# Sums of the modulation weights: three GpSimd instructions a tile, or two on VectorE

## The chip, the core and the metric

The kernel runs on one core of a Trainium2 chip. The metric is the device time of one execution in microseconds (us); smaller is better. A core has TensorE (PE, matrix products; PEld is its loading of weights), VectorE (DVE), ScalarE (ACT), GpSimd (POOL), and SyncE (SP), whose queue issues nearly all transfers here. Each engine takes its own instructions in order; engines wait for each other by semaphores.

## What is computed

A transformer of four layers (attention of three kinds, a memory attention, SwiGLU) runs over 256 positions, and behind it a second block of two layers. The second block scales, shifts and gates its layers by a modulation vector, which depends on a small input c alone:

```python
c_act = jax.nn.silu(c.astype(jnp.float32))          # 1 x 1024
def hybrid_layer(x, c_act, norm_g, w_ada, b_ada, w_in, w_out, pos):
    mod = c_act @ w_ada + b_ada                     # w_ada: 1024 x 3072, for each of two layers
    shift, scale, gate = jnp.split(mod, 3, axis=-1)
    h = rms_norm(x, norm_g) * (1.0 + scale[:, None, :]) + shift[:, None, :]
    ...
```

The change concerns the product c_act @ w_ada.

## The kernel before

All weights are fp32 and pass through the core once. `load_w` (L249) loads a tile of 128x1024 (512 KB) into a buffer `raw` (a pool of 5 buffers), splits it into a high part `wh` (ACT, L262) and a low part `wl` (DVE, L264), and PE multiplies with both (three products each). `wh` and `wl` have eight buffers each; a buffer is free when PE has used it.

A layer of the first block goes through projections and attention, the out projection with a layer norm (`add_norm`: L481 and L482 on DVE sum and take statistics, L455 and L448 give v, L450 on POOL takes its power -1/2, L462 and L463 on DVE apply it; PE then transposes the result in L368), gate and up in six groups (`units_T`, L436 to L438, eight weight tiles in each but the first; ACT applies silu in L1135, DVE multiplies with up in L1139, ACT and DVE split the product in L1142 and L1143), and down (L295 to L297). Down takes over accumulator banks, one of which is free only when L1139 has read it.

The modulation is computed on the side, during gate and up of the four layers. w_ada is loaded in 48 tiles `raw` of 256 rows by 512 columns (kq is the tile's number in a chunk of four, ch the chunk, of which there are six to each of two modulation layers). In the order of loads two such tiles follow each of the six gate and up groups. `load_ada` (L1205) issues the load on SP, and POOL multiplies both halves of the tile with silu(c), one value to each partition, and adds them to the chunk's sum `ada`:

```python
cb = self.cact[:, kq * 2:kq * 2 + 2].unsqueeze(2).to_broadcast([P, 2, 512])
nc.gpsimd.tensor_tensor(rv, rv, cb, op=ALU.mult)                     # L1216
if kq == 0:
    nc.gpsimd.tensor_tensor(acc, rv[:, 0, :], rv[:, 1, :], op=ALU.add)    # L1218
else:
    nc.gpsimd.tensor_tensor(acc, acc, rv[:, 0, :], op=ALU.add)       # L1220
    nc.gpsimd.tensor_tensor(acc, acc, rv[:, 1, :], op=ALU.add)       # L1221
```

After a chunk's fourth tile, DVE transposes and reduces the sum (L1227, L1228). The buffer `raw` is free for the next load when the last reader has ended; SP takes its loads in order, so one that waits for a buffer holds those behind it. A scheduler orders each engine's instructions by its own estimate when the program is built.

Of the kernel before, what the change touches and what calls it, by code (L numbers as in the profile page):

```python
# [15 lines left out]
ALU = mybir.AluOpType  # L16
AX = mybir.AxisListType

P = 128
# [101 lines left out]
class _Net:  # L121
# [1083 lines left out]
    def load_ada(self, l, ch, kq):  # L1205

        nc, I = self.nc, self.I
        c0 = ch * 512
        if kq == 0:
            self.ada_acc = self.s2([512], name="ada")  # L1210
        acc = self.ada_acc
        raw = self.rawp.tile([P, 1024], F32, name="raw", tag="t")
        rv = raw.rearrange("p (k n) -> p k n", n=512)
        nc.sync.dma_start(rv, I["w_ada_2"][l, kq * 256:kq * 256 + 256, c0:c0 + 512].rearrange("(k p) n -> p k n", p=P))
        cb = self.cact[:, kq * 2:kq * 2 + 2].unsqueeze(2).to_broadcast([P, 2, 512])
        nc.gpsimd.tensor_tensor(rv, rv, cb, op=ALU.mult)  # L1216
        if kq == 0:
            nc.gpsimd.tensor_tensor(acc, rv[:, 0, :], rv[:, 1, :], op=ALU.add)  # L1218
        else:
            nc.gpsimd.tensor_tensor(acc, acc, rv[:, 0, :], op=ALU.add)  # L1220
            nc.gpsimd.tensor_tensor(acc, acc, rv[:, 1, :], op=ALU.add)  # L1221
        if kq < 3:
            return

        def finish():
            t = self.s2([512], name="adaT")
            nc.vector.transpose(t, acc)  # L1227
            nc.vector.tensor_reduce(self.adared[l][:, ch * 16:ch * 16 + 16], t.rearrange("p (b i) -> p b i", i=32),  # L1228
                                    axis=AX.X, op=ALU.add)
            if ch < 5:  # L1230
                return
            ps = self.at_bank()
            nc.tensor.matmul(ps[0:32, 0:96], self.fold, self.adared[l], start=True, stop=True)
            col = self.adain[l]
            nc.vector.tensor_tensor(col, ps[0:32, 0:96], col, op=ALU.add)
            scale = col[:, 32:64]
            nc.vector.scalar_tensor_tensor(scale, scale, 1.0, self.adag[l], op0=ALU.add, op1=ALU.mult)
            nc.sync.dma_start(self.rows[l].rearrange("o (k p) -> p (o k)", p=32), col)

        self.put_off(12, finish)  # L1240
# [349 lines left out]
```

## Time and profile before

| | |
|---|---|
| runs | 1643.12 us median of 3 (1642.08 to 1646.56) |
| profiled execution | 1647.93 us, its span 1646.2 us |
| PE, matrix products | busy 1589.9 us, 97% of the span |
| DVE | 1119.7 us, 68% |
| ACT | 825.2 us, 50% |
| POOL | 390.6 us, 24% |
| granted clock of TensorE | 0.989 of 2.4 GHz over the span |
| transfers | 299.98 MB, 182 GB/s in the mean |

The profile comes from one execution. Times in it count from the start of the span. A wait is put down to the instruction that ended last before the waiting one could go on. A busy share is a mean over parts with different limits, so what counts for the time is which engine waits in which part, and for whom.

### The profile page before, as it was taken

The numbers are of one execution on the slowest core, as the hardware profiler recorded it, in microseconds if no ns is written. First come the engines' busy times: TensorE is split into PE (matmuls) and PEld (weight loads), VectorE is DVE, ScalarE is ACT, GpSimd is POOL, SyncE is SP. The second block draws the span as 40 slices with busy tenths as digits, with TensorE's granted clock in tenths as the row PEclk, the third lists the DMA queues.
The fourth block names the chain that finished last, engine by engine and source line by source line (L and its number), as shares of the span: only waits on it lengthen the run. The fifth ranks groups of instructions, "written<-read, shape, count | busy, mean of one in ns | idle before, by whom it ended". The sixth has DMA issues, their size and how long they took to land.

```text
span 1646.2 us, 27453 instructions
## 1 busy us (share of the span) xinstructions
PE 1589.9 (97%) x10840; PEld 1427.3 (87%) x10840; DVE 1119.7 (68%) x1496; ACT 825.2 (50%) x1281; POOL 390.6 (24%) x358
## 2 busy tenths in 40 slices
PE   8899999999999998999999999999999899999997
PEld 7788799978889998889799988887999778887976
DVE  7963777757567876575578847865788566486475
ACT  5575544444454443366444534655444345655572
POOL 2210343401122442022335500123254011001002
PEclk9999999999999999999999999999999999999999
DMA  8736477655456665663366666533676567344721
GB/s 288 213 110 198 147 251 240 216 182 170 126 166 192 229 224 194 179 191 124 123 220 212 240 211 216 150 103 122 219 239 233 146 202 268 102 154 145 226 78 39
DMA packets 200529, 299.98 MB, mean 182 GB/s; under 512 B 26576, under 2 KB 84304, under 8 KB 200400
## 3 DMA queue, kind: packets, MB, share of 16 engines
q1 hardware_dynamic: 200400, 298.23, 56.7%
q8 instruction: 85, 1.39, 0.3%
q14 instruction: 44, 0.36, 0.1%
HBM read 295.54 MB, written 2.65 MB: 181 GB/s over the span
## 4 chain that ended last, share of the span: by engine, by line
PE 44%; DVE 3%; DMA 2%; POOL 2%; ACT 2%; issue 1%; POOLq 0%; SPq 0%; ACTq 0%; DVEq 0%
PE mm L295 7%; PE mm L296 7%; PE mm L297 7%; PE mm L438 6%; PE mm L437 6%; PE mm L436 6%; PE at L368 2%; DVE wl L264 1%; DMA raw<-w_ada 1%; DMA raw<-w_down 1%; PE at L810 1%; ACT wh L262 1%; PE at L1388 1%; POOL raw L1216 0%; PE at L1401 0%
## 5 line engine op out<-in xcount | busy, mean ns | idle before, releaser
L264 DVE TENSOR_TENSOR wl<-raw,wh 128x1024 fp32r<-128x1024 f32 (+2 forms) x488 | 656.8, 1360 | 310.4 <-ACT wh L262 298.6
L262 ACT ACTIVATE wh<-raw 128x1024 fp32r<-128x1024 f32 (+2 forms) x488 | 509.5, 1048 | 528.1 <-DMA raw<-w_gate_up 201.9
L436 PE MATMUL mm<-xh,wh 128*128 128x256 f32 x1472 | 416.9, 283 | 0.0
L438 PE MATMUL mm<-xh,wl 128*128 128x256 f32 x1472 | 416.6, 283 | 0.0
L437 PE MATMUL mm<-xl,wh 128*128 128x256 f32 x1472 | 416.5, 283 | 0.0
L295 PE MATMUL mm<-wh,xh 128*128 128x256 f32 (+3 forms) x912 | 294.6, 324 | 1.7 <-ACT xh L408 1.7
L296 PE MATMUL mm<-wl,xh 128*128 128x256 f32 (+3 forms) x912 | 289.4, 318 | 2.3 <-DVE wl L264 2.3
L297 PE MATMUL mm<-wh,xl 128*128 128x256 f32 (+3 forms) x912 | 288.3, 317 | 0.0
L437 PEld LDWEIGHTS mm<-xl,wh 128*128 128x128 f32 x1472 | 282.6, 192 | 0.1
L436 PEld LDWEIGHTS mm<-xh,wh 128*128 128x128 f32 x1472 | 282.6, 192 | 0.1
L438 PEld LDWEIGHTS mm<-xh,wl 128*128 128x128 f32 x1472 | 282.6, 192 | 0.0
L295 PEld LDWEIGHTS mm<-wh,xh 128*128 128x128 f32 x912 | 174.6, 192 | 13.4 <-ACT xh L408 2.3
L296 PEld LDWEIGHTS mm<-wl,xh 128*128 128x128 f32 x912 | 175.0, 192 | 12.9 <-DVE wl L264 2.7
L297 PEld LDWEIGHTS mm<-wh,xl 128*128 128x128 f32 x912 | 174.4, 192 | 8.3 <-DVE xl L409 0.2
L1216 POOL TENSOR_TENSOR raw<-raw,cact 128x1024 f32<-128x1024 f32 x48 | 104.7, 2187 | 301.1 <-DMA raw<-w_ada 233.3
L450 POOL TENSOR_TENSOR r<-v,mhalf 128x1 f32<-128x1 f32 (+1 forms) x26 | 24.6, 947 | 628.9 <-DVE v L448 608.3
L295 PE MATMUL mm<-wh,hh 128*128 128x512 f32 x320 | 126.4, 395 | 0.0
L296 PE MATMUL mm<-wl,hh 128*128 128x512 f32 x320 | 125.6, 392 | 0.0
L297 PE MATMUL mm<-wh,hl 128*128 128x512 f32 x320 | 125.5, 392 | 0.0
L652 POOL TENSOR_TENSOR t<-nat,rc 128x64 f32<-128x64 f32 (+1 forms) x44 | 25.5, 580 | 276.6 <-ACT nat L173 189.0
L295 PE MATMUL mm<-wh,Th 128*128 128x512 f32 x160 | 66.3, 414 | 14.2 <-DVE h L1139 13.4
L295 PEld LDWEIGHTS mm<-wh,hh 128*128 128x128 f32 x320 | 61.1, 191 | 13.0
(229 smaller groups left out, 2121.7 us busy)
## 6 DMA issues: line engine op xcount, KB each, us to landing
raw<-w_gate_up SPq DMA_DIRECT2D x176, 512.0 KB, 4.9
raw<-w_down SPq DMA_DIRECT2D x88, 512.0 KB, 5.6
raw<-w_in SPq DMA_DIRECT2D x64, 512.0 KB, 4.3
raw<-w_out SPq DMA_DIRECT2D x48, 512.0 KB, 4.6
raw<-w_ada SPq DMA_DIRECT2D x48, 512.0 KB, 5.7
raw<-w_in_a SPq DMA_DIRECT2D x44, 512.0 KB, 4.8
raw<-w_in_c SPq DMA_DIRECT2D x20, 512.0 KB, 5.1
raw<-w_mem_kv SPq DMA_DIRECT2D x16, 512.0 KB, 4.3
```

Of the source, the lines that this page charges most:

```text
L262: nc.scalar.activation(hi[:, 0:w], raw[:, 0:w], AF.Copy)
L264: nc.vector.tensor_tensor(lo[:, 0:w], raw[:, 0:w], hi[:, 0:w].bitcast(F32), op=ALU.subtract)
L295: nc.tensor.matmul(ps, xh, wh, start=first and i == 0, stop=False)
L296: nc.tensor.matmul(ps, xh, wl, start=False, stop=False)
L297: nc.tensor.matmul(ps, xl, wh, start=False, stop=last and i == len(wt) - 1)
L368: self.nc.tensor.transpose(ps[:, j * P:(j + 1) * P], nat[:, j * P:(j + 1) * P], self.ident)
L436: nc.tensor.matmul(ps, wh[:, cols], xh, start=i == 0 and a == 0 and c % 2 == 0, stop=False)
L437: nc.tensor.matmul(ps, wh[:, cols], xl, start=False, stop=False)
L438: nc.tensor.matmul(ps, wl[:, cols], xh, start=False, stop=end and c % 2 == 1)
L450: self.nc.gpsimd.tensor_tensor(r, v, self.mhalf[:, 0:n], op=ALU.pow)
L652: eng.tensor_tensor(a, xv[:, :, 0:16], bc(self.rc, 0, 16), op=ALU.mult)
L1216: nc.gpsimd.tensor_tensor(rv, rv, cb, op=ALU.mult)
```

## The change

The sums move from POOL to DVE, and a multiplication and an addition become one instruction: for each half of a tile, ada = raw * silu(c) + ada, and for the first half of a chunk the product alone. A tile is no longer overwritten by its product.

```diff
-        cb = self.cact[:, kq * 2:kq * 2 + 2].unsqueeze(2).to_broadcast([P, 2, 512])
-        nc.gpsimd.tensor_tensor(rv, rv, cb, op=ALU.mult)
-        if kq == 0:
-            nc.gpsimd.tensor_tensor(acc, rv[:, 0, :], rv[:, 1, :], op=ALU.add)
-        else:
-            nc.gpsimd.tensor_tensor(acc, acc, rv[:, 0, :], op=ALU.add)
-            nc.gpsimd.tensor_tensor(acc, acc, rv[:, 1, :], op=ALU.add)
+        for j in range(2):
+            k = kq * 2 + j
+            cb = self.cact[:, k:k + 1]
+            if k == 0:
+                nc.vector.tensor_scalar(acc, rv[:, j, :], cb, None, op0=ALU.mult)
+            else:
+                nc.vector.scalar_tensor_tensor(acc, rv[:, j, :], cb, acc, op0=ALU.mult, op1=ALU.add)
```

On PE, ACT and SP the order of the instructions is the same in both programs. POOL's order is that of before without the lines of `load_ada`. On DVE the scheduler places the new instructions (L1219 the plain product, L1221 the others) among the others. The first place is the end of the attention and the out projection's norm, here in the first layer (p is the softmax, oTl the low part of the attention's output); this is a piece of the difference on DVE:

```order
 L796 TENSOR_TENSOR p<-p,rz 128x512 x2
+L1219 TENSOR_SCALAR ada<-raw,cact 128x512
+L1221 SCALAR_TENSOR_TENSOR ada<-raw,cact,ada 128x512
 L761 TENSOR_TENSOR oTl<-at,oTh 128x256
 L481 SCALAR_TENSOR_TENSOR x<-x,mm_2066 128x512
-L482 BN_STATS st<-x 128x6
+L1221 SCALAR_TENSOR_TENSOR ada<-raw,cact,ada 128x512
+L482 BN_STATS st<-x 128x6
+L1221 SCALAR_TENSOR_TENSOR ada<-raw,cact,ada 128x512
 L481 SCALAR_TENSOR_TENSOR x<-x,mm_2136 128x512
```

The four instructions of a layer's first two w_ada tiles stand ahead of and among the first half's sum and statistics.

The second place is the end of gate and up in the last of the four layers, on DVE, before (the first two L1139 belong to the last group but one, the next two to the last group; the seven L264 between them are for w_down tiles, the one ahead of L1143 for the last gate and up tile):

```order
L1139 TENSOR_TENSOR h<-h,mm_13713 128x512
L1139 TENSOR_TENSOR h<-h,mm_13714 128x512
L264 TENSOR_TENSOR wl<-raw,wh 128x1024
L1143 TENSOR_TENSOR hl<-h,hh 128x512 x2
L264 TENSOR_TENSOR wl<-raw,wh 128x1024 x7
L1139 TENSOR_TENSOR h<-h,mm_13981 128x512
L1139 TENSOR_TENSOR h<-h,mm_13982 128x512
```

The same place on DVE now:

```order
L1139 TENSOR_TENSOR h<-h,mm_13680 128x512
L1221 SCALAR_TENSOR_TENSOR ada<-raw,cact,ada 128x512
L1139 TENSOR_TENSOR h<-h,mm_13681 128x512
L264 TENSOR_TENSOR wl<-raw,wh 128x1024
L1143 TENSOR_TENSOR hl<-h,hh 128x512
L1221 SCALAR_TENSOR_TENSOR ada<-raw,cact,ada 128x512
L1143 TENSOR_TENSOR hl<-h,hh 128x512
L1221 SCALAR_TENSOR_TENSOR ada<-raw,cact,ada 128x512
L264 TENSOR_TENSOR wl<-raw,wh 128x1024
L1221 SCALAR_TENSOR_TENSOR ada<-raw,cact,ada 128x512
L264 TENSOR_TENSOR wl<-raw,wh 128x1024 x6
L1139 TENSOR_TENSOR h<-h,mm_13947 128x512
```

The four instructions of the layer's last two w_ada tiles stand between the products of the last group but one and the first two w_down tiles.

## Rows read from the trace of the kernel before

**Rows 1.** Waits of PE: waiter, releaser, us in total, times, longest us.

```profile
PE mm L295 <- DVE h L1139: 13.4, 4, 4.9
...
PE at L368 <- DVE x L463: 5.6, 3, 2.0
```

**Rows 2.** Waits of SP, with the same columns.

```profile
SPq L258 <- POOL ada L1221: 175.0, 28, 8.4
```

**Rows 3.** Chain of waits, layer 2's out norm: start us, us, what.

```profile
803.54 1.90 POOL raw L1216
...
805.51 1.29 POOL ada L1218
...
806.82 3.58 DMA raw<-w_ada
...
815.51 0.97 POOL r L450
...
816.50 0.76 DVE x L463
```

**Rows 4.** Timeline there, DVE: start, us, instruction, count, [idle before <-releaser].

```profile
806.32 0.42 DVE L761 TENSOR_TENSOR oTl<-at,oTh 128x256 fp32r<-128x256 f32 x1 [3.50 <-ACT oTh L760]
...
808.66 0.69 DVE L481 SCALAR_TENSOR_TENSOR x<-x,mm 128x512 f32<-128x512 f32 x1 [1.92 <-PE mm L297]
...
811.38 0.69 DVE L481 SCALAR_TENSOR_TENSOR x<-x,mm 128x512 f32<-128x512 f32 x1 [1.30 <-PE mm L297]
...
813.08 0.15 DVE L448 TENSOR_SCALAR v<-mv 128x1 f32<-128x1 f32 x1
```

**Rows 5.** Timeline, the end of gate and up in layer 3.

```profile
1265.06 1.28 DVE L1139 TENSOR_TENSOR h<-h,mm 128x512 f32<-128x512 f32 x2
...
1265.51 1.89 POOL L1216 TENSOR_TENSOR raw<-raw,cact 128x1024 f32<-128x1024 f32 x1 [12.51 <-DMA raw<-w_ada]
...
1275.95 1.29 POOL L1221 TENSOR_TENSOR ada<-ada,raw 128x512 f32<-128x512 f32 x1
...
1277.27 0.37 SPq L258 DMA_DIRECT2D raw<-w_down  x1
...
1291.10 0.79 PE L295 MATMUL mm<-wh,Th 128*128 128x512 f32 x1 [4.86 <-DVE h L1139]
```

**Rows 6.** Stretches: us, busy PE, PEld, DVE, ACT, POOL (instructions); PEclk, DMA, GB/s.

```profile
331.00:336.00 5.00, 4.90 (x16) 3.96 (x17) 4.47 (x7) 1.26 (x2) 0.00 (x0) 0.70 0.84 291
646.00:651.00 5.00, 5.00 (x12) 3.91 (x13) 4.14 (x6) 1.01 (x2) 0.00 (x0) 0.50 0.83 263
817.00:822.00 5.00, 4.56 (x17) 3.68 (x18) 5.00 (x7) 1.99 (x3) 0.00 (x0) 0.67 0.60 193
1291.00:1296.00 5.00, 4.90 (x12) 3.84 (x13) 4.47 (x7) 1.26 (x2) 0.00 (x0) 0.50 0.84 286
```

**Rows 7.** The same view for gate and up: layer 2, and all four layers.

```profile
840.00:950.00 110.00, 110.00 (x919) 110.00 (x919) 87.34 (x61) 49.80 (x56) 54.81 (x28) 1.00 0.68 229
...
sum 420.00, PE 420.00 PEld 419.96 DVE 330.80 ACT 188.31 POOL 205.66; mean PE 105.00 PEld 104.99 DVE 82.70 ACT 47.08 POOL 51.41
```

**Rows 8.** Groups, 840 to 950 us: count | busy us, mean ns | idle before, releasers.

```profile
L264 DVE TENSOR_TENSOR wl<-raw,wh 128x1024 fp32r<-128x1024 f32 x39 | 65.1, 1690 | 21.0 <-ACT wh L262 18.8 <-PE mm L438 1.4
L1143 DVE TENSOR_TENSOR hl<-h,hh 128x512 fp32r<-128x512 f32 x8 | 15.7, 2006 | 0.0
L1139 DVE TENSOR_TENSOR h<-h,mm 128x512 f32<-128x512 f32 x8 | 5.1, 681 | 0.0
...
L1216 POOL TENSOR_TENSOR raw<-raw,cact 128x1024 f32<-128x1024 f32 x10 | 22.1, 2210 | 59.8 <-DMA raw<-w_ada 50.2 <-DVE wl L264 9.5
```

**Rows 9.** Groups, 342 to 372 us (down of layer 0, POOL idle).

```profile
L264 DVE TENSOR_TENSOR wl<-raw,wh 128x1024 fp32r<-128x1024 f32 x14 | 17.2, 1226 | 15.7 <-ACT wh L262 14.4
```

**Rows 10.** Groups over the span, apart by shape.

```profile
L463 DVE SCALAR_TENSOR_TENSOR x<-x,r,bc 128x512 f32<-128x512 f32 x32 | 22.6, 749 | 1.3 <-POOL r L450 1.3
...
L1540 DVE TENSOR_SCALAR xw<-xw,r 128x512 f32<-128x512 f32 x1 | 0.5, 486 | 0.8 <-POOL r L1273 0.8
```

## The prediction

> **What bounds the kernel now.** I read the waits of TensorE first. TensorE (PE) sets the time: in the four stretches in which gate and up are multiplied it is busy 420.0 of 420.0 us [rows 7], so work on another engine costs time only where PE waits for it. Two waits are of interest, and both end on VectorE (DVE): 13.4 us in four pieces on the product h of L1139, at the start of each layer's down part, and 5.6 us in three pieces on the normalised x of L463, after the out projection [rows 1]. Next I looked at what stands behind each.
>
> After the out projection (layer 2 shown, layers 0 and 3 alike) the chain of waits runs through GpSimd (POOL): the first w_ada tile lands, POOL multiplies it and adds, only when that add ends (806.80) does the second w_ada load start, it is multiplied and added twice, and only then, at 815.51, POOL takes the power for the layer norm, which lets L463 start at 816.50 [rows 3]. The value v that the power reads was there at 813.23 [rows 4]. So the norm waits 2.3 us for sums that nobody needs then.
>
> At the end of gate and up (layer 3 shown) POOL is late: the first tile of the last pair is there at 1265.51, when its multiplication starts, the second's last add ends at 1277.24, and 0.03 us later SP issues a w_down load that waited for its buffer [rows 5]. The weights behind it go through ACT and DVE in order; L1139 stands behind them on DVE, and PE, which goes on at 1291.10, has waited 4.86 us for it [rows 5]. Over the run SP waits 175.0 us, 28 times, for POOL's last add before it may load a weight [rows 2].
>
> PE pays for these waits twice. Beside four of them (the down starts of layers 0, 1 and 3, and layer 2's norm) the granted clock is at its lower level (1.2 GHz, share 0.50 of 2.4 GHz) for a while: means of 0.70, 0.50, 0.67 and 0.50 over 5 us each [rows 6]. At half the clock, 5 us at 0.50 is 2.5 us of lost work (12 matmuls end in it where 24 would). The four give 1.5 + 2.5 + 1.65 + 2.5 = 8.2 us.
>
> **The change part by part.** It takes all sums off POOL: 48 tiles with three instructions each. It puts 96 instructions on DVE: 12 plain products and 84 multiply-adds on 128x512 with a scalar per partition and, in all but the first of a chunk, the sum of the one before. The nearest rows are 0.486 us for the plain product (L1540) and 0.749 us for the multiply-add (L463, also in a chain) [rows 10]: 12 x 0.486 + 84 x 0.749 = 68.7 us of DVE time. Below, it could hardly be less than the plain product's 0.486 (46.7 us); above, 2.006 us, L1143's mean beside a busy POOL [rows 8], would make 193 us, but POOL's big work is gone, so I take 0.749.
>
> **DVE in the gate and up part** costs nothing, because it gives back more than it takes. In 840 to 950 us DVE is busy 87.3 us [rows 7]. There L264 takes 1.690 us, but 1.226 where POOL rests [rows 8, 9]; L1143, which reads two operands in SBUF, takes 2.006, while L1139 of the same size, with one operand in PSUM, takes 0.681 [rows 8]. Back come 39 x 0.464 = 18.1 and 8 x 1.325 = 10.6, together 28.7 us. The ten tiles of this stretch [rows 8] add 2 x 0.486 + 18 x 0.749 = 14.5. DVE goes to 73.1 of 110 us. Cover is lost only if the 28.7 stay; that is a rival below. The Trainium skill (SBUF — State Buffer, § SBUF: two separate sides) says that VectorE instructions with two SBUF inputs and GpSimd instructions hold one port pair in turn, each for a whole instruction, the loser blocked. By that rule all of the 28.7 us come back; by chance scatter none would; the trace agrees with the rule as far as L1139, with an input in PSUM, is not stretched.
>
> **The down starts.** In DVE's new order the last pair's four instructions stand around the two L1139 and the two L1143 of the group before, with two L264 between. From L1139 at 1265.06 [rows 5] I count 2 x 0.681 + 2 x 0.681 + 2 x 1.226 + 4 x 0.749 = 8.2 us, so both buffers are free by 1273.3 instead of 1277.24: 3.9 us earlier, and the first tile's, after its second sum, already at about 1269.8. A wait that shrinks by 3.9 us leaves 4.9 - 3.9 = 1.0 of the longest and nothing of those of 3.9 or less. I leave 0.4 more for the others, 1.4 of 13.4 in all, and count 12.0 gained; the bounds are 0 (rival A) and 13.4. What is late next is the release of weight tiles by PE itself, which is no loss. The instructions queued behind the new waits are the second L1139 and an L264 whose weights PE needs some 20 us later (a group of eight weight tiles lasts 23 us); ACT's L1142 waits for that L1139, with the same slack.
>
> **The norm after out.** Two of the sums now stand on DVE ahead of L761 and two around the first L482. The first tile is there at 803.54 (POOL's start before [rows 3]); its two sums end at 804.8, in time in which DVE was idle (it had waited 3.50 us when L761 came at 806.32 [rows 4]); so the second load starts 2.0 us earlier than 806.82 and, with the same 3.58 us [rows 3], lands by 808.4. The next sums run after L481 (808.66 to 809.35) [rows 4], so they don't wait; the second L481 starts at 811.6 instead of 811.38. The power then starts at v, about 813.5, under the two L462 (1.5 us), and L463 at 815.0 instead of 816.50. Each of the three waits loses 1.5 us: 4.4 of 5.6 (0.4 each stay). SP's queue is the same, but the weights that stood behind the second tile's buffer are issued when the fourth sum ends, 811.6 instead of 815.5; nobody waits for them here, so I count nothing.
>
> **The clock.** If the waits shrink to a microsecond or less, the low stretches beside them have no cause left: 8.2 us; if they stay all the same, 0. Between the ends I take 8.2, since the short waits mostly have none beside them: of the three norm waits, at most 2.0 us long, one has (817), of the four down starts three have.
>
> Sum: 12.0 + 4.4 + 8.2 = 24.6 us. The profiled execution took 1647.9 us (span 1646.2 and 1.7 around it), which would go to 1623.3. The median of the runs is 4.8 us below the profiled one, so I subtract from the median: 1643.1 - 24.6 = **1618.5 us**.
>
> **Rivals.**
> A: the w_down loads are late for their own sake (five land together, and the burst is limited by the transfers, not by when buffers come free). Then the down starts and their low clock stay, and only 4.4 + 1.65 us are gained: 1637.1. For it speaks that after 1277.27 the loads go out in a burst; against it, that SP issues the first of them 0.03 us after POOL's last add.
> B: the waits go but the clock still falls, for other reasons: 1643.1 - 16.4 = 1626.7. The fourfold coincidence with the waits speaks against it.
> C, slower: DVE becomes the bound of the gate and up part, because its long instructions are not POOL's doing. Then DVE has 87.3 + 14.5 = 101.8 us of work in 110, and if all of its 21.0 us of waits before L264 [rows 8] stay too, the stretch lasts 122.8: 12.8 us more, 48.9 over the 420 us, and with the gains 1643.1 + 48.9 - 24.6 = 1667.4. It decides where less than 12.8 of the 28.7 us come back (below that PE starts to wait), and the result is slower than before where less than 6.4 do. Against it: 0.681 beside 2.006 for the same size. The Trainium skill (Perfetto Trace Analysis, § Optimizing Scalar/DVE Operations) allows work to go from a saturated DVE to GpSimd, which would make this change a step back; it adds that between these two it might not help, because they share a port. By the first half of it rival C would be right, by the second the forecast.
> That the change does not move the sums is excluded by the order of the built program: POOL has none of them left.
>
> **How the numbers follow.** A change of under 0.3% (4.9 us) can't be told from none, so faster means below 1638.2. Forecast, with a half or more of the down gain: 0.70. A: 0.13, of which I give 0.05 to a result within 0.3%. B: 0.10. C: 0.05, slower. Something that cancels most of the gain: 0.02, within 0.3%. Faster 0.70 + 0.08 + 0.10 = 0.88, same 0.07, slower 0.05. The best case takes all of 13.4 + 5.6 + 8.2 = 27.2 us, 1615.9; 3 us below that for small waits without a row here gives the low end, 1613. The high end is A, 1637. A range to there leaves out C, the rest, half of A and the best tail: about 0.18.
>
> **What would show it.** Right: POOL's busy time falls by more than half; L1143 near 0.69 and L264 near 1.23 us in the gate and up part; no wait of SP on POOL; PE's wait on L1139 under 2 us in total, on L463 about 1; clock near 1.00 where the four stretches were. Wrong: L1139 still waited for by 2 us or more in any layer (A), low clock without a wait (B), PE waiting for wl in the middle of gate and up (C), or L481 or L463 later than PE needs them because a sum in front of them waits for w_ada.

## The result and the profile after

The changed kernel takes 1620.95 us (median of 4 runs, 1620.18 to 1622.91), the kernel before 1644.84 us (1642.08 to 1647.08, 4 runs on the same chip): a ratio of 0.9842, 95% interval 0.9813 to 0.9871, or 23.9 us less. Forecast were 1618.5 us and 24.6 us less.

The engines' busy time over the span of 1618.1 us, from the page of the kernel after:

```profile
PE 1581.2 (98%) x10840; PEld 1423.0 (88%) x10840; DVE 1066.7 (66%) x1592; ACT 822.9 (51%) x1281; POOL 139.7 (9%) x226
```

POOL falls from 390.6 to 139.7 us. DVE gets 96 instructions more and is still busy for 53.0 us less than before. PE executes the same 10840 matmuls in 8.7 us less, which is the clock: of down's matmuls 12 end in 5 us at a granted clock of 0.50 [rows 6], and 24 at 1.00 (the stretch 326 to 331, shown with the step on the clock below).

The longest waits of PE now (waiter, releaser, us in total, times, longest us):

```profile
PE at L368 <- DMA x<-x: 8.1, 2, 5.4
PE at L368 <- DVE xw L1442: 6.4, 4, 2.2
PE mm L296 <- DVE wl L264: 2.3, 1, 2.3
```

Neither wait of [rows 1] is in the list any more: 13.4 us on h and 5.6 us on x have gone altogether. The three at its head stand at the start of the program, in the norms of the second block and in the first layer. The waits of SP, the same columns:

```profile
SPq L258 <- DVE wl L264: 826.3, 360, 23.4
...
SPq L258 <- DVE ada L1221: 43.9, 36, 3.2
```

SP waits for POOL's adds nowhere. Where [rows 2] had 175.0 us in 28 waits of up to 8.4 us for the last add, it now waits 43.9 us in 36 pieces of at most 3.2 us for the last sum on DVE. The long line on L264 is the ordinary pacing of the loads by PE.

The gate and up part of layer 2 (the stretch of [rows 7], some 18 us earlier now; busy time of PE, PEld, DVE, ACT, POOL, then PEclk, DMA share, GB/s):

```profile
822.00:932.00 110.00, 110.00 (x920) 110.00 (x919) 75.55 (x84) 53.47 (x61) 0.00 (x0) 1.00 0.79 252
```

and the groups of DVE in it (count | busy us, mean ns | idle before, releasers):

```profile
L264 DVE TENSOR_TENSOR wl<-raw,wh 128x1024 fp32r<-128x1024 f32 x42 | 51.4, 1224 | 34.3 <-ACT wh L262 33.9
L1221 DVE SCALAR_TENSOR_TENSOR ada<-raw,cact,ada 128x512 f32<-128x512 f32 x18 | 13.4, 746 | 0.1
L1139 DVE TENSOR_TENSOR h<-h,mm 128x512 f32<-128x512 f32 x8 | 5.5, 682 | 0.1
L1143 DVE TENSOR_TENSOR hl<-h,hh 128x512 fp32r<-128x512 f32 x8 | 5.3, 685 | 0.0
```

Against [rows 8], L264 goes from 1690 to 1224 ns and L1143 from 2006 to 685, the same as L1139, which has not moved (681 and 682). DVE has 84 instructions where it had 61 and is busy 75.6 us where it was 87.3.

The out norm of layer 2, the place of [rows 3, 4] (start us, us, engine, instruction, count, [idle before <-releaser]):

```profile
795.31 0.69 DVE L481 SCALAR_TENSOR_TENSOR x<-x,mm 128x512 f32<-128x512 f32 x1 [1.88 <-PE mm L297]
...
798.03 0.69 DVE L481 SCALAR_TENSOR_TENSOR x<-x,mm 128x512 f32<-128x512 f32 x1
...
799.73 0.15 DVE L448 TENSOR_SCALAR v<-mv 128x1 f32<-128x1 f32 x1
799.96 0.99 POOL L450 TENSOR_TENSOR r<-v,mhalf 128x1 f32<-128x1 f32 x1 [16.82 <-DVE v L448]
801.12 1.41 DVE L463 SCALAR_TENSOR_TENSOR x<-x,r,bc 128x512 f32<-128x512 f32 x2
```

POOL has idled for 16.82 us when v comes, and takes the power 0.23 us after v's start. Before, 2.43 us lay between v (813.08) and the power (815.51).

The end of gate and up in layer 3, the place of [rows 5]:

```profile
1239.17 0.68 DVE L1139 TENSOR_TENSOR h<-h,mm 128x512 f32<-128x512 f32 x1
...
1245.83 0.74 DVE L1221 SCALAR_TENSOR_TENSOR ada<-raw,cact,ada 128x512 f32<-128x512 f32 x1
...
1252.43 1.23 DVE L264 TENSOR_TENSOR wl<-raw,wh 128x1024 fp32r<-128x1024 f32 x1 [1.65 <-ACT wh L262]
1255.31 1.23 DVE L264 TENSOR_TENSOR wl<-raw,wh 128x1024 fp32r<-128x1024 f32 x1 [1.66 <-ACT wh L262]
...
1262.21 1.41 DVE L1139 TENSOR_TENSOR h<-h,mm 128x512 f32<-128x512 f32 x2
```

From the first L1139 to the end of the last sum it is 7.4 us; before it was 12.2 (1265.06 to 1277.24). The L264 for the w_down tiles then come one every 2.88 us, each after 1.65 us of idle time (1252.43 and 1255.31). DVE has time to spare there, and the next L1139 is not held up.

### The profile page after: what moved, and what is told of

It is laid out like the page before. It is cut to its first block, busy times and chain, and to the rows that moved or that the text cites. A ratio compares the mean times of both kernels' runs of the same rounds, so it can differ in the third digit from the quotient of the medians.

```text
span 1618.1 us, 27388 instructions
## 1 busy us (share of the span) xinstructions
PE 1581.2 (98%) x10840; PEld 1423.0 (88%) x10840; DVE 1066.7 (66%) x1592; ACT 822.9 (51%) x1281; POOL 139.7 (9%) x226
## 4 chain that ended last, share of the span: by engine, by line
PE 50%; DVE 3%; ACT 1%; issue 1%; POOL 1%; POOLq 0%; ACTq 0%; DVEq 0%
PE mm L295 8%; PE mm L297 8%; PE mm L296 8%; PE mm L437 6%; PE mm L436 6%; PE mm L438 6%; PE at L368 2%; PE at L810 1%; DVE wl L264 1%; PE at L1388 1%; PE at L734 1%; PE at L1401 0%; PE at L1354 0%; PE at L1318 0%; POOL xw L1264 0%
## 5 line engine op out<-in xcount | busy, mean ns | idle before, releaser
L264 DVE TENSOR_TENSOR wl<-raw,wh 128x1024 fp32r<-128x1024 f32 (+2 forms) x488 | 588.9, 1215 | 349.9 <-ACT wh L262 342.3
L262 ACT ACTIVATE wh<-raw 128x1024 fp32r<-128x1024 f32 (+2 forms) x488 | 509.8, 1049 | 514.5 <-PE mm L437 219.7
L297 PEld LDWEIGHTS mm<-wh,hl 128*128 128x128 f32 x320 | 60.1, 188 | 12.6
L296 PEld LDWEIGHTS mm<-wl,hh 128*128 128x128 f32 x320 | 60.1, 188 | 12.2
```

Source lines behind the costliest of these rows:

```text
L262: nc.scalar.activation(hi[:, 0:w], raw[:, 0:w], AF.Copy)
L264: nc.vector.tensor_tensor(lo[:, 0:w], raw[:, 0:w], hi[:, 0:w].bitcast(F32), op=ALU.subtract)
L296: nc.tensor.matmul(ps, xh, wl, start=False, stop=False)
L297: nc.tensor.matmul(ps, xl, wh, start=False, stop=last and i == len(wt) - 1)
```

## The experiments

Theory **buffers**: the down starts waited because POOL gave the last pair's buffers back late, so the w_down loads were issued late; the norm waited because the power stood behind sums on POOL. Theory **stretching**: the gain comes from DVE's instructions that a busy POOL no longer draws out. Rival C of the prediction is the dark side of the second: DVE full, and slower. The median of the kernel before lies at 1647.4 to 1648.3 us in these comparisons, so a difference to it is taken within each.

**The last pair alone.** The kernel before, with this branch in `load_ada` (kq 2 and 3 of a layer's last chunk):

```diff
+        if ch % 3 == 2 and kq >= 2:
+            for j in range(2):
...
+                    nc.vector.scalar_tensor_tensor(acc, rv[:, j, :], cb, acc, op0=ALU.mult, op1=ALU.add)
+        else:
...
```

> The kernel before, with one part of the change alone: of each layer's six pairs of w_ada tiles only the last is summed on VectorE, the other five stay on GpSimd. Theory 'buffers' (the down starts wait because GpSimd gives the last pair's buffers back late, so the w_down loads are issued late): the four waits of TensorE on h (13.4 us) go, the low clock beside three of them (1.5 + 2.5 + 2.5 us) too, the norm's waits stay: about 1644.8 - 19.9 = 1625. Theory 'stretching' (the gain comes because VectorE's instructions are no longer drawn out by a busy GpSimd): 40 of 48 tiles are still on GpSimd beside gate and up, VectorE stays drawn out there, and at most a sixth of the 19.9 us comes: about 1641 or more.

Measured: 1626.7 against 1648.3 us, ratio 0.9875 (0.9827 to 0.9922), 21.6 us less. A wait of PE:

```profile
PE at L368 <- DVE x L463: 4.3, 3, 1.7
```

and one of SP (L1230 is L1221 of before):

```profile
SPq L258 <- POOL ada L1230: 128.3, 20, 8.4
```

No wait on h is left, while the norm's three stay. SP has lost 8 of its 28 waits on POOL, two a layer, and the waits on h went with them. In this build one L1142 and one L262 of each layer also change places on ACT. So the gain does not come from stretching all along gate and up: 40 tiles are still on POOL, and L1143 still takes 1449 ns in the mean over the run (1697 before, 685 after). But POOL is now idle beside the last pair, so DVE is no longer drawn out just ahead of L1139 either. This run alone can't tell late buffers from stretching at that one place; the run with six buffers does.

**The first pair alone.** The same with `ch % 3 == 0 and kq < 2`.

> The kernel before, with only the first pair of each layer summed on VectorE (the pair that lands around the out projection's norm). If the norm waits because its power stands behind these sums on GpSimd, the three waits on L463 (5.6 us) and the low clock beside layer 2's (1.65 us) go, the four on h stay: about 1644.8 - 7.3 = 1637.5. If the norm is late for another reason (the statistics, the power itself): 1645, and the waits on L463 stay.

Measured: 1640.3 against 1648.3 us, ratio 0.9949 (0.9920 to 0.9978), 8.0 us less. The wait of PE on L463 is gone; the other one is not:

```profile
PE mm L295 <- DVE h L1139: 20.5, 4, 6.4
```

This profile is of the slowest of ten executions (1648.8 us), so its 20.5 us can't be set against the median; what it shows is that the two waits are separate.

**Both pairs**, `ch % 3 == 0 and kq < 2 or ch % 3 == 2 and kq >= 2`: 16 of 48 tiles.

> The kernel before, with the first and the last pair of each layer summed on VectorE, the four pairs between them on GpSimd as before. Theory 'two places': the gain of the change lies in these two pairs, the other 32 tiles bring nothing, because their late buffers are made up for while TensorE still has weights: 1621, within 3 us of the kernel after, no wait on h or L463. Theory 'all tiles' (a VectorE no longer drawn out brings something of its own): 5 us or more slower than the kernel after, 1626 or above.

Measured: 1619.5 against 1647.5 us, ratio 0.9833 (0.9788 to 0.9878), 28.0 us less; the two runs above add up to 29.6. The interval holds the ratio of the whole change, 0.9842. The gate and up part of layer 2, the view of [rows 7], and after it two groups of DVE there, as in [rows 8]:

```profile
822.00:932.00 110.00, 110.00 (x919) 110.00 (x919) 84.55 (x67) 52.19 (x60) 44.89 (x22) 1.00 0.71 245
```

```profile
L264 DVE TENSOR_TENSOR wl<-raw,wh 128x1024 fp32r<-128x1024 f32 x41 | 62.3, 1532 | 23.3 <-ACT wh L262 15.6 <-PE mm L437 7.2
L1143 DVE TENSOR_TENSOR hl<-h,hh 128x512 fp32r<-128x512 f32 x8 | 13.6, 1730 | 0.0
```

POOL works for 44.9 us, L1143 takes 1730 ns, and PE is busy for 110.00 of 110 us all the same. So DVE's relief beside the other 32 tiles brings nothing, and these could have stayed on POOL.

**Six buffers, nothing moved.** The kernel before with one constant changed:

```diff
-RAW_BUFS = 5
+RAW_BUFS = 6
```

> The kernel before with six raw buffers for five, all sums on GpSimd. Theory 'buffers': a buffer that GpSimd gives back late is needed one load later, and a weight tile lasts TensorE 2.9 us; each of the four waits on h (2.9, 4.5, 1.1, 4.9 us) shrinks by 2.9 us, to 0 + 1.6 + 0 + 2.0 = 3.6, and with part of the clock beside them 12 to 16 us are gained: 1629 to 1633. Theory 'transfers' (the w_down loads are late for their own sake): the waits stay, 1645.

With the sixth buffer the scheduler also places one weight tile's split otherwise on ACT and DVE at the start of each layer's gate and up, and on POOL the second product of a layer's first pair; SP issues some loads earlier. DVE's order at the end of gate and up is that of before.

Measured: 1634.8 against 1647.5 us, ratio 0.9925 (0.9900 to 0.9949), 12.7 us less. Two waits of PE:

```profile
PE at L368 <- DVE p L796: 8.6, 7, 1.7
...
PE mm L295 <- DVE h L1139: 3.5, 3, 1.3
```

The wait on h comes to 3.5 us where 3.6 was expected, with all sums on POOL and DVE as drawn out as before (L1143 1682 ns over the run, 1697 before). It is as drawn out at the very place, too. The two L1143 at the end of layer 3, before the change and then here:

```profile
1268.40 3.48 DVE L1143 TENSOR_TENSOR hl<-h,hh 128x512 fp32r<-128x512 f32 x2
```

```profile
1260.82 3.48 DVE L1143 TENSOR_TENSOR hl<-h,hh 128x512 fp32r<-128x512 f32 x2
```

So the stretching stays and most of the wait goes: it hung on the late buffers. PE's wait on x (5.6 us before) is gone as well, which the expectation did not count: the second tile of the first pair no longer needs the first one's buffer, and POOL's sums end sooner. A wait on the softmax p (8.6 us against 1.1) stands against the gain, and the timeline of layer 3's attention shows where it is from:

```profile
1125.56 4.19 POOL L1216 TENSOR_TENSOR raw<-raw,cact 128x1024 f32<-128x1024 f32 x2 [4.68 <-DMA raw<-w_ada]
...
1125.99 4.31 DVE L796 TENSOR_TENSOR p<-p,rz 128x512 f32<-128x512 f32 x2
```

With a buffer more, w_ada lands while DVE still multiplies p, and two products that take 0.7 us each over the run of before take 4.31 us beside POOL. The 5.6 us that went uncounted and the 7.5 that came nearly cancel, so the total met its expectation in part by luck.

**A queue and a buffer of its own for w_ada**, the sums on POOL:

```diff
-        raw = self.rawp.tile([P, 1024], F32, name="raw", tag="t")
+        raw = self.adap.tile([P, 1024], F32, name="adaraw", tag="t")
...
-        nc.sync.dma_start(rv, I["w_ada_2"][l, kq * 256:kq * 256 + 256, c0:c0 + 512].rearrange("(k p) n -> p k n", p=P))
+        nc.gpsimd.dma_start(rv, I["w_ada_2"][l, kq * 256:kq * 256 + 256, c0:c0 + 512].rearrange("(k p) n -> p k n", p=P))
```

> The kernel before, all sums on GpSimd as they were, but the w_ada tiles go to a buffer of their own and are loaded by GpSimd's own queue, so that no weight load waits for GpSimd. Theory 'buffers': the four waits on h and the low clock beside three of them go (19.9 us), though VectorE and GpSimd still run side by side; the sums still stand ahead of the power, so the norm's waits stay at 5 us or more: about 1625. Theory 'stretching': nothing changes for VectorE, the waits on h stay: 1645, or more by what the loads cost GpSimd.

Measured: 1641.8 against 1648.3 us, ratio 0.9968 (0.9944 to 0.9992), 6.5 us less, where about 20 were expected. The waits on h are gone as expected. The norm's have tripled, and PE waits 2.8 us on a sum of the attention (L749) as it did not before:

```profile
PE at L368 <- DVE x L463: 16.7, 12, 2.8
```

The timeline of one norm shows why:

```profile
515.82 0.15 DVE L448 TENSOR_SCALAR v<-mv 128x1 f32<-128x1 f32 x1
...
516.65 1.61 POOL L1221 TENSOR_TENSOR ada<-ada,adaraw 128x512 f32<-128x512 f32 x1
518.56 0.74 POOL L1214 DMA_DIRECT2D adaraw<-w_ada  x1 [0.30 <-POOL ada L1221]
519.32 0.57 POOL L450 TENSOR_TENSOR r<-v,mhalf 128x1 f32<-128x1 f32 x1
```

v is there at 515.97 us, but the power has to wait for POOL's sum and for the issue of its next load, until 519.32. So POOL's place in the norm's chain costs by the length of what is queued ahead of it. This run also moves POOL's work against DVE's (L1143 796 ns over the run), so by itself it could not rule out stretching; the run with six buffers does that.

**Contention put back.** The kernel after, with POOL doing as much as before on a buffer that nobody reads. A copy of 128x1 on DVE tells it that a tile is there:

```diff
+        nc.vector.tensor_copy(tok, raw[:, 0:1])
...
+        nc.gpsimd.tensor_tensor(sr.rearrange("p (k n) -> p k n", n=P), self.ident.unsqueeze(1).to_broadcast([P, 8, P]),
+                                tok.unsqueeze(2).to_broadcast([P, 8, P]), op=ALU.mult)
+        for _ in range(1 if kq == 0 else 2):
+            nc.gpsimd.tensor_tensor(sr[:, 0:512], sr[:, 0:512], sr[:, 512:1024], op=ALU.add)
```

> The kernel after, with GpSimd doing beside it as much as before: for each w_ada tile one product of 128x1024 and one or two sums of 128x512, on a buffer of its own and read by nobody; it starts when the tile has landed and holds none of the weights' buffers. Theory 'buffers': the waits on h stay away although VectorE is drawn out again (about 102 of 110 us busy in the middle of gate and up); the power stands behind the extra work again, so the norm's waits (5.6 us) and the clock beside one (1.65 us) come back: about 1628. Theory 'stretching': the waits on h come back with their clock: 1621 + 19.9 + 7.3 = 1648, and if VectorE becomes the bound of gate and up (the rival that ends slower), up to 1667.

Measured: 1674.5 against 1648.3 us, ratio 1.0162 (1.0110 to 1.0215). With late buffers of POOL as the only cause 1628 was expected; this is 46.5 us more. Its control has the copies and the same order on PE, ACT, SP and DVE, but without POOL's extra work:

> The control for the kernel after with GpSimd's extra work: all its small copies on VectorE (one value for each partition and w_ada tile, which told GpSimd that the tile was there), with the same order on every other engine, but no extra work on GpSimd. If it was GpSimd's work that brought the waits on h back (32.8 us), they are gone here: 1621 and at most 5 us for 48 copies of 0.15 us. If it was the copies, which wait for w_ada on VectorE ahead of other work: the waits on h stay near 30 us and the time near 1674.

Measured: 1621.65 us, as the kernel after. So the 52.8 us between the two are POOL's work (the two stand in different comparisons, whose kernels before are 0.8 us apart). The copies are in both: how much of this POOL's work would cost without copies that wait for w_ada was not tested. The waits of PE on h and x in the first:

```profile
PE mm L295 <- DVE h L1139: 32.8, 4, 9.3
PE at L368 <- DVE x L463: 6.8, 4, 2.5
```

DVE's groups in its gate and up part of layer 2 (850 to 960 us; L1228 is the multiply-add, L1216 the copy):

```profile
L264 DVE TENSOR_TENSOR wl<-raw,wh 128x1024 fp32r<-128x1024 f32 x37 | 57.4, 1576 | 4.2 <-ACT wh L262 4.1
L1228 DVE SCALAR_TENSOR_TENSOR ada<-raw,cact,ada 128x512 f32<-128x512 f32 x15 | 16.4, 1091 | 0.0
L1143 DVE TENSOR_TENSOR hl<-h,hh 128x512 fp32r<-128x512 f32 x7 | 12.4, 1795 | 0.0
L1139 DVE TENSOR_TENSOR h<-h,mm 128x512 f32<-128x512 f32 x8 | 5.3, 678 | 0.0
...
L1216 DVE COPY tok<-raw 128x1 f32<-128x1 f32 x9 | 1.4, 151 | 13.8 <-DMA raw<-w_ada 13.8
```

The control, the same view, 835 to 945 us:

```profile
L264 DVE TENSOR_TENSOR wl<-raw,wh 128x1024 fp32r<-128x1024 f32 x40 | 49.0, 1225 | 31.3 <-ACT wh L262 31.0
```

Ahead of L264 DVE waits 31.3 us in the control for weights that PE paces, which is its spare time; beside a busy POOL 4.2 us of that are left. It is busy for 91.9 of the 110 us there, 73.8 in the control, and most of what remains (13.8 us, 4.8 in the control) its copy stands in its order for a w_ada tile that itself came late, with weights queued behind. The tiles come late because buffers come free late, and now it is DVE that holds them. The waits of SP on DVE's readers of w_ada:

```profile
SPq L258 <- DVE ada L1228: 73.9, 32, 4.4
...
SPq L258 <- DVE tok L1216: 41.9, 12, 6.5
```

In the control these two are 38.0 and 5.5 us. At the end of a layer PE waits up to 9.3 us for L1139. Rival C foresaw such a slower kernel, 1667.4 us for the 1674.5 here, but by another way: PE was to wait inside gate and up, which would last 12.8 us longer in 110. The four parts of gate and up (215 to 330, 535 to 650, 851 to 966 and 1191 to 1306 us) in the view of [rows 7]:

```profile
sum 460.00, PE 458.63 PEld 458.36 DVE 397.03 ACT 201.98 POOL 225.63; mean PE 114.66 PEld 114.59 DVE 99.26 ACT 50.50 POOL 56.41
```

PE loses only 1.4 us there. It loses 32.8 us at the down starts, 6.8 in the norms, and is busy for 10.5 us more than in the control (1593.7 against 1583.2), which is the clock. The Trainium skill (SBUF — State Buffer, § SBUF: two separate sides) has VectorE instructions with two SBUF inputs and GpSimd take turns at one port pair; the trace agrees, with L1143 at 1795 and L1139, which reads PSUM, at 678.

**Where it has to be put back.** The same extra work beside all pairs but the last of each layer, and beside the last alone:

```diff
+        if ch % 3 != 2 or kq < 2:
```

> The kernel after with GpSimd's extra work beside all pairs but the last of each layer. Theory 'the end': VectorE drawn out costs only where its work stands ahead of the w_down weights, so the waits on h fall from 32.8 us to 3 or less and what is left is the norm's: 1621 + 7.3, about 1630. Theory 'all along': VectorE falls behind over the whole gate and up part and carries that to its end: the waits on h stay at 15 us or more, 1650 or above.

Measured: 1649.4 us, 27.7 more than the control (ratio to before 1.0020, 0.9992 to 1.0048). Waits of PE:

```profile
PE mm L295 <- DVE h L1139: 11.2, 4, 3.7
PE at L368 <- DVE x L463: 7.8, 4, 3.0
```

The time is that of 'all along', the wait on h lies between the two expectations. The other half tells more (the condition turned round):

> The kernel after with GpSimd's extra work beside the last pair of each layer alone, the other half of what the run with the work beside all pairs but the last did (waits on h 11.2 us there, 32.8 us with both). If the two halves add up: waits on h 32.8 - 11.2 = 21.6 us, and with the clock beside them about 1674.5 - 1649.4 = 25 us more than the control: 1647. If VectorE must be behind already for the last pair to cost anything: waits on h 5 us or less, 1630 or below. The norm's power has no extra work ahead of it, so no wait on L463 in either case.

Measured: 1621.65 us, the same as the control (ratio to before 0.9847, 0.9818 to 0.9876), with no wait on h, although the multiply-adds are drawn out there too:

```profile
L1229 DVE SCALAR_TENSOR_TENSOR ada<-raw,cact,ada 128x512 f32<-128x512 f32 x84 | 70.8, 842 | 0.3
```

So the halves don't add up: 27.7 and 0.0 alone, 52.8 together. Work beside the last pair costs 25.1 us on top of the work beside the others, and nothing without it. That DVE must be late already is the reading that fits, and the expectation had it as its second case.

**Can more be had?** Six buffers with both versions.

> The kernel with the first and the last pair of each layer on VectorE, and six raw buffers for five. If late buffers were all that was left of the cause, nothing remains to be gained, since no wait on h or L463 is left: 1619.5, within 3 us. If the attention's weights gain by the sixth buffer too: below 1616. If GpSimd's sums move into the attention with it, as in the kernel before with six buffers (waits on p, 8.6 us): up to 1626.

> The kernel after with six raw buffers for five. If late buffers were all of the cause, nothing remains: 1621, within 3 us, and GpSimd has no sums that could move into the attention, so no waits on p come as in the kernel before with six buffers. If the sixth buffer has a worth of its own: below 1617.

Measured: 1619.25 us (ratio 0.9812, 0.9771 to 0.9853) and 1621.57 us (0.9826, 0.9791 to 0.9861). The sixth buffer, worth 12.7 us before, is worth nothing that these runs can tell once the late sums of the first and last pairs are gone. No version was found that beats the kernel after by more than the runs can tell.

## Why the prediction came out right, step by step

- **What bounds the kernel** held: only the waits of PE counted, and the clock beside them. The run with both pairs shows it best, where DVE is busy for 9.0 us more in the stretch than in the kernel after, at no cost.
- **The cost of the sums**: 5.5 us for the 12 plain products (458 ns each) and 62.6 for the 84 multiply-adds (746 ns), 68.1 where 68.7 was counted. The row of L463 was the right one to take.
- **DVE in gate and up**: 75.6 of 110 us where 73.1 were counted; the stretch holds 42 L264 instead of 39, which is 3.7 of it. Both drawn-out instructions came back to their quiet times. The prediction said that cover is lost if they do not: with the same sums, POOL busy beside them and the copies added, the kernel is slower than before (contention put back).
- **The down starts**: the mechanism was right, the term too small, 12.0 counted and 13.4 come. It let the last sum come 3.9 us sooner; it came 4.8 us sooner (7.4 instead of 12.2 us after L1139), about the length of the longest wait, 4.86. The step that was off is the sum of 8.2 us, which adds whole durations; instructions that follow each other start up to 0.1 us before the one ahead has ended.
- **The norm after out**: right too, and too small, 4.4 counted and 5.6 come. It gave each wait 1.5 us; L463 starts 5.8 us after the first L481 instead of 7.8, which is 2.0, and the longest wait was 2.0. Two steps were off. The delay of the second L481 was put at 0.2 us and is 0.0 (2.72 us after the first in both), so v comes 4.42 us after the first L481, as before. And from v's start to L463 the prediction had 1.7 us (813.3 to 815.0), where it is 1.4 (799.73 to 801.12). The two L462 cover the power, as it said.
- **The clock**: right in its four places, with 1.7 us given back in a fifth. Granted clock (the number behind the five busy times) in the places of [rows 6], and in a place at the start of the second block:

```profile
326.00:331.00 5.00, 5.00 (x24) 4.13 (x23) 3.96 (x6) 1.34 (x3) 0.00 (x0) 1.00 0.58 202
635.00:640.00 5.00, 5.00 (x24) 4.14 (x23) 3.87 (x5) 0.96 (x2) 0.00 (x0) 1.00 0.63 227
802.00:807.00 5.00, 4.96 (x26) 4.10 (x26) 5.00 (x6) 3.94 (x5) 0.00 (x0) 1.00 0.42 125
1264.00:1269.00 5.00, 5.00 (x24) 4.14 (x23) 3.82 (x5) 0.91 (x2) 0.00 (x0) 1.00 0.54 187
1339.00:1344.00 5.00, 4.87 (x18) 3.89 (x19) 2.12 (x4) 1.23 (x3) 0.00 (x0) 0.66 0.90 343
```

  In all PE is busy 8.7 us less, 8.2 were counted. These are not all the same microseconds: from 74 to 82 us, ahead of all w_ada tiles, the granted clock is 0.57 before and 0.79 now, which is 1.8 us. The prediction's reason, that without the waits the low level has no cause left, is too strong, as the last section shows.
- **The sum**: 24.6 forecast; the spans differ by 28.1 us, the profiled executions (1647.93 and 1620.18) by 27.8, the medians by 23.9. Waits of 13.4 + 5.6, a wait of 1.7 us on the attention's input (`ACT xh L408`) that went without having been counted, and 8.7 of busy time make 29.4; small waits elsewhere take 1.3 back. The profiled execution of before was 3.1 us above its median and that of after 0.8 below its own, which is the step from 27.8 to 23.9. So that the total is only 0.7 us off is partly luck: between the profiled executions the parts came 3.2 us larger than counted, and a gain read from an execution slower than the median was taken off the median whole. The forecast time is 2.4 us low, 1.7 of it because the median of before rose from 1643.12 to 1644.84 us with a fourth run.
- **The rivals**: A is out, since the waits on h shrink to a quarter with one buffer more and go with the last pair's engine alone. B is out for the four places by the rows above. C did not come: DVE is busy 75.6 of 110 us, and the drawn-out times were POOL's doing. With POOL's work put back a slower kernel near C's price came, but not by C's way (PE loses 1.4 us inside gate and up, not 48.9), so the price was not confirmed. The Trainium skill (Perfetto Trace Analysis, § Optimizing Scalar/DVE Operations) says that with a saturated VectorE it may make sense to move work, even to GpSimd, and warns that between these two it might not help. The trace agrees with the warning: the sums on POOL cost DVE more time (1119.7 us busy) than the sums on DVE (1066.7). But VectorE was not saturated here, and the time was gained by earlier buffers.

## What to carry to other kernels

Work on the side that reads from a shared pool of buffers costs what it holds, at the moment when the next stage's loads come round to that buffer: find the few tiles where this happens (16 of 48 here) before moving all of them, and try one buffer more first. Before giving work to an engine off the path, look how much idle time paced by the bound engine it has left: here DVE took 9.0 us more at no cost with both pairs, and with 4.2 of 31.3 us of this idle time left the kernel lost 52.8. A short instruction of a norm on an in-order engine is as late as what is queued ahead of it.

## What was not expected of the hardware

- The price of contention is not additive: POOL's extra work beside the last pairs (8 of 48 tiles) cost 0.0 us by itself and 25.1 on top of that beside the other 40, when DVE had little spare time left (4.2 of 31.3 us).
- The clock does not answer a wait in the same way each time. At the start of the second block PE waits for L1442 at the same place in both kernels. First the kernel before, its wait and the stretch behind it, then the kernel after (its stretch stands above):

```profile
1368.78 1.32 PE L368 MATMUL at<-ident,xw 128*128 128x128 f32 x8 [2.22 <-DVE xw L1442]
...
1367.00:1372.00 5.00, 3.21 (x17) 2.37 (x18) 2.77 (x4) 1.40 (x3) 0.94 (x2) 1.00 0.97 374
```

```profile
1339.13 1.72 PE L368 MATMUL at<-ident,xw 128*128 128x128 f32 x8 [2.23 <-DVE xw L1442]
```

  The wait is 2.22 and 2.23 us, the granted clock 1.00 (2.4 GHz throughout) and 0.66 (at 1.2 GHz for part of it). In all thirteen profiles of this case this wait is 2.2 to 2.3 us, and seven of them show the lower level behind it. Nor does the lower level need a wait: in the control the granted clock from 478 to 488 us, in the attention of layer 1, is 0.66 with PE busy for 10.00 of the 10 us, and the kernel after has 1.00 there (474 to 484). What decides this stays open. In the places of [rows 6] the lower level cost 1.5 to 2.5 us of 5, so a clock term worked out from waits should have bounds of that size for each of them.
